# Rotary embedding over 16 batches: which batches form a pair, and where the first tile and the tables are loaded

## The chip, the cores and the metric

The kernel runs on one core of a Trainium2 chip. The metric is the device time of one execution in microseconds (us); before the change the median of three runs is 167.71 us (167.61 to 167.97). The core has five engines that this text calls PE (matrix products), DVE (vector), ACT (scalar), POOL (GpSimd) and SP (sync; here it only issues transfers). Transfers between DRAM and the on-chip memory run on 16 DMA engines. A transfer is put on the queue of the engine that issues it: SP's queue is q1 in the profile, ACT's is q10.

## The reference

A rotary position embedding. `x` is 16 batches of 512 rows of 16 heads by 64 numbers, 33.5 MB in float32; `cos` and `sin` are 512 by 32, 64 KB each, and are the same for all batches and heads.

```python
def reference(x, cos, sin, num_heads):
    batch, seq, dim = x.shape                    # 16, 512, 1024
    head_dim = dim // num_heads                  # 64
    half_dim = head_dim // 2
    x = x.reshape(batch, seq, num_heads, head_dim)
    x1, x2 = x[..., :half_dim], x[..., half_dim:]
    cos = cos[None, :, None, :]
    sin = sin[None, :, None, :]
    rotated = np.concatenate([x1 * cos - x2 * sin, x1 * sin + x2 * cos], axis=-1)
    return rotated.astype(np.float32)
```

Every number of `x` is read once and every number of the output is written once.

## The kernel before

**Tiles.** The work is cut into ten tiles (L40, L41). Tiles 0, 1, 8 and 9 hold one batch each (0, 1, 14 and 15): 4 rows of 1024 numbers on each of 128 partitions, 2 MB, each partition reading 16 KB in one piece. Tiles 2 to 7 hold two batches each (2 and 3, 4 and 5, up to 12 and 13): 8 rows per partition, 4 MB. In a pair, partition 2s belongs to the first batch and partition 2s + 1 to the second, and each reads 8 rows that lie together in DRAM, 32 KB in one piece. Two neighbouring batches are 2 MB apart. The 64 rows in all, in the order of the tiles, are numbered u = 0 to 63.

**Memory.** The tiles live in a ring of 40 rows, `x_sb` (RING, L43). Tiles 0 to 5 fill it. Tiles 6 to 9 take the places of earlier tiles: tile 6 that of tiles 0 and 1, tile 7 that of tile 2, and tiles 8 and 9 that of tile 3. The result of a row overwrites the row in the ring, and is stored from there.

**One row.** A row takes three steps. The product with cos goes to one of three buffers in PSUM, `t1_ps` (DVE, L313). The product of the swapped halves with sin (negative for the first half) goes to one of six buffers, `t2_sb`; POOL does it (L277), except in row 3 of each pair, where DVE does it (L306). Then the two are added: by DVE, straight into the ring (L324), or, in three rows of eight, by PE, which adds `t2_sb` to what stands in `t1_ps` by a product with the identity (L232), and ACT copies the sum to the ring (L198). DVE's product for row u waits until the buffer of row u - 3 is free: for ACT's copy of that row, or for its add.

**Tables.** `cos` and `sin` are loaded into `stage` with 4 rows on each partition, 512 bytes per partition and table. DVE copies cos to PSUM (L284) and waits for it before its first product. ACT makes the table of sin with both signs, `s1_sb` (L189, L190), and POOL waits for it before its first product. For the pairs, PE spreads both tables to 8 rows per partition by a product with a 0/1 matrix, `pick` (L215), and ACT makes `s2_sb` from the result (L193, L194). The spread relies on the order of the partitions in a pair, first and second batch in turn.

**Queues.** SP issues the first half of tile 0 (2 rows per partition, 1 MB), then cos, then sin (L165 to L167), and then the stores, each when the last row of its tile is done (L171, L173). ACT issues the second half of tile 0 (L177), the loads of tiles 1 to 5 (L183, L162), and then waits for sin. The semaphore of tile 0 counts 32, 16 for each half (L275, L299). The loads of tiles 6 to 9 stand between ACT's copies, at rows 17, 25 and 33 (`later`, L186, LAG being 10); ahead of each, ACT waits until the tiles whose place is taken have been stored (`sem_out`). What follows in ACT's program, the later copies among it, comes after that wait.

Of the kernel before, what the change touches and what calls it, by code (L numbers as in the profile page):

```python
# [6 lines left out]
def bass_split_heads_rope_kernel(  # L7
# [4 lines left out]
    num_heads: bass.AP,  # L12
    out: bass.AP,
):

# [6 lines left out]
    batch, seq, dim = x.shape  # L24
# [4 lines left out]
    R1 = seq // P  # L29
    R2 = 2 * R1  # L30
# [6 lines left out]
    COPY = mybir.ActivationFunctionType.Copy  # L37


    singles = (0, 1, batch - 2, batch - 1)  # L40
    tiles = [(b, R1 if b in singles else R2) for b in range(batch) if b in singles or b % 2 == 0]  # L41
    NT = len(tiles)
    RING = 5 * R2  # L43

    rows = [(t, r) for t, (_, n) in enumerate(tiles) for r in range(n)]
    NU = len(rows)
    EARLY = (NU - RING) // R2

# [17 lines left out]
    LAG = 10  # L66

    with ExitStack() as stack:
        x_sb = stack.enter_context(nc.sbuf_tensor([P, RING, H, 2, HALF], fp32))
        t2_sb = stack.enter_context(nc.sbuf_tensor([P, NT2, H, 2, HALF], fp32))  # L70
        stage = stack.enter_context(nc.sbuf_tensor([P, 2, R1 * HALF], fp32))
# [8 lines left out]
        sem_in = [stack.enter_context(nc.semaphore(f"in{t}")) for t in range(NT)]  # L80
        sem_out = [stack.enter_context(nc.semaphore(f"out{k}")) for k in range(EARLY)]
        sem_rest = stack.enter_context(nc.semaphore("rest"))
        sem_cos = stack.enter_context(nc.semaphore("cos"))
        sem_sin = stack.enter_context(nc.semaphore("sin"))
# [22 lines left out]
        x1 = x.rearrange("b (s r) d -> b s (r d)", r=R1)  # L107
# [4 lines left out]

        def in_dram(single, pairs, t):
            b, n = tiles[t]
            return single[b] if n == R1 else pairs[:, b:b + 2, :]

        def in_sbuf(t):
            b, n = tiles[t]
            k = b * R1 % RING
            return x_sb[:, k:k + n].rearrange("p n h t d -> p (n h t d)")  # L120

        def where(u):
# [24 lines left out]

        def stores_of(k):

            return sum(b * R1 // R2 == k for b, _ in tiles)  # L150

        HR = R1 // 2

        def load_half(eng, i):

            eng.dma_start(  # L156
                x_sb[:, i * HR:(i + 1) * HR].rearrange("p n h t d -> p (n h t d)"),
                x1[0, :, i * HR * dim:(i + 1) * HR * dim],
            ).then_inc(sem_in[0], 16)

        def load(eng, t):
            eng.dma_start(in_sbuf(t), in_dram(x1, x2, t)).then_inc(sem_in[t], 16)  # L162

        def on_sync(sp):
            load_half(sp, 0)  # L165
            for i, (table, sem) in enumerate(((cos, sem_cos), (sin, sem_sin))):
                sp.dma_start(stage[:, i, :], table.rearrange("(s r) d -> s (r d)", r=R1)).then_inc(sem, 16)  # L167
            for u in range(NU):
                t, r, k = where(u)
                if r == tiles[t][1] - 1:  # L170
                    wait_added(sp, u)  # L171
                    k = u // R2
                    sp.dma_start(in_dram(o1, o2, t), in_sbuf(t)).then_inc(sem_out[k] if k < EARLY else sem_rest, 16)  # L173
            sp.wait_ge(sem_rest, 16 * sum(stores_of(k) for k in range(EARLY, NU // R2)))

        def on_scalar(ae):
            load_half(ae, 1)  # L177
            later = {}
            for t, (b, n) in enumerate(tiles):
                if t == 0:  # L180
                    continue
                if b * R1 + n <= RING:
                    load(ae, t)  # L183
                else:

                    later.setdefault((b * R1 - RING) // R2 * R2 + R2 - 1 + LAG, []).append(t)  # L186
            ae.wait_ge(sem_sin, 16)
            sv = stage[:, 1, :].rearrange("s (r d) -> s r d", d=HALF)
            ae.activation(s1_sb[:, :, 0, :], sv, COPY, scale=-1.0)  # L189
            ae.activation(s1_sb[:, :, 1, :], sv, COPY).then_inc(sem_s, 1)  # L190
            ae.wait_ge(sem_t, 2)
            s2 = s2_sb[:].rearrange("p (k r) t d -> p k r t d", r=R1)
            ae.activation(s2[:, :, :, 0, :], pair_ps[:, :, 1, :, :], COPY, scale=-1.0)  # L193
            ae.activation(s2[:, :, :, 1, :], pair_ps[:, :, 1, :, :], COPY).then_inc(sem_s, 1)  # L194
            for u in range(NU):
                if PE2[u]:
                    ae.wait_ge(sem_e, n_pe[u])
                    ae.activation(xs[:, u % RING, :], t1_ps[:, u % NT1, :], COPY).then_inc(sem_a, 1)  # L198
                for t in later.get(u, ()):
                    k = (tiles[t][0] * R1 - RING) // R2  # L200
                    ae.wait_ge(sem_out[k], 16 * stores_of(k))
                    load(ae, t)

# [38 lines left out]
        def on_gpsimd(pl):  # L242
            pl.memset(ident[:], 1.0).then_inc(sem_i, 1)  # L243
            pl.wait_ge(sem_i, 1)
            pl.affine_select(  # L245
                out=ident[:],
                in_=ident[:],
                compare_op=mybir.AluOpType.is_equal,
                fill=0.0,
                base=0,  # L250
                pattern=[[-1, P]],
                channel_multiplier=1,
            ).then_inc(sem_i, 1)

            pl.memset(pick[:], 1.0).then_inc(sem_g, 1)
            pl.wait_ge(sem_g, 1)
            for k in range(2):
                pl.affine_select(  # L258
                    out=pick[:, k],
                    in_=pick[:, k],  # L260
                    compare_op=mybir.AluOpType.is_equal,
                    fill=0.0,
                    base=-k,
                    pattern=[[-2, P // 2], [0, 2]],
                    channel_multiplier=1,
                ).then_inc(sem_g, 1)
            for u in range(NU):
                if V2[u]:
                    continue
                t, r, k = where(u)  # L270
                if (t, r) == (0, 0):
                    pl.wait_ge(sem_s, 1)
                if (t, r) == (2, 0):
                    pl.wait_ge(sem_s, 2)
                pl.wait_ge(sem_in[t], 32 if t == 0 else 16)  # L275
                wait_t2_free(pl, u)
                pl.tensor_tensor(  # L277
                    t2_sb[:, u % NT2, :, :, :], swapped(k), over_heads(s_of(t, r)), mult
                ).then_inc(sem_p, 1)

        def on_vector(ve):
            ve.memset(zero[:], 0.0).then_inc(sem_z, 1)  # L282
            ve.wait_ge(sem_cos, 16)
            ve.tensor_copy(c1_ps, stage[:, 0, :].rearrange("s (r d) -> s r d", d=HALF)).then_inc(sem_c, 1)  # L284
            ve.wait_ge(sem_c, 1)
            ve.wait_ge(sem_w, NT1 * EH)

            def pair_tables():
                ve.wait_ge(sem_s, 2)
                row = pair_ps[:, V_ROW // R1, 1, V_ROW % R1, :]  # L290
                ve.tensor_scalar_mul(v_ps[:, 0, :], row, -1.0).then_inc(sem_c, 1)
                ve.tensor_copy(v_ps[:, 1, :], row).then_inc(sem_c, 1)

            first_v = V2.index(True)

            def mul(u):
                t, r, k = where(u)
                if r == 0:
                    ve.wait_ge(sem_in[t], 32 if t == 0 else 16)  # L299
                if (t, r) == (2, 0):  # L300
                    pair_tables()
                if u == first_v:
                    ve.wait_ge(sem_c, 3)
                if V2[u]:
                    wait_t2_free(ve, u)
                    ve.tensor_tensor(t2_sb[:, u % NT2, :, :, :], swapped(k), over_heads(v_ps), mult)  # L306
                if u >= NT1:
                    v = u - NT1
                    if PE2[v]:
                        ve.wait_ge(sem_a, n_pe[v])  # L310
                    else:
                        ve.wait_ge(sem_v, n_comb[v])
                ve.tensor_tensor(  # L313
                    t1_ps[:, u % NT1, :].rearrange("p (h d) -> p h d", d=HALF),
                    x_sb[:, k, :, :, :].rearrange("p h t d -> p (h t) d"),
                    c_of(t, r)[:, None, :].broadcast_to([P, 2 * H, HALF]),
                    mult,
                ).then_inc(sem_m, 1)

            def comb(u):  # L320
                t, r, k = where(u)
                ve.wait_ge(sem_m, u + 1)
                ve.wait_ge(sem_p, n_pool[u])  # L323
                ve.tensor_tensor(  # L324
                    xs[:, k, :],
                    t1_ps[:, u % NT1, :],
                    t2_sb[:, u % NT2, :, :, :].rearrange("p h t d -> p (h t d)"),
                    add,
                ).then_inc(sem_v, 1)

            for u in range(NU + LEAD):
                if u < NU:
                    mul(u)
                if u >= LEAD and not PE2[u - LEAD]:
                    comb(u - LEAD)
# [39 lines left out]
```

## Time and profile before

| | |
|---|---|
| median of three runs | 167.71 us |
| the profiled run | 167.97 us, span 166.6 us |
| bytes read and written | 33.69 MB and 33.55 MB |
| mean rate over the span | 404 GB/s |
| POOL busy | 136.4 us of the span |
| DVE busy | 130.1 us |
| first multiply on POOL begins | 24.7 us |
| first store issued | 35.4 us |
| last store issued | 160.2 us |

The span runs from the first to the last instruction of the profiled execution; the run's own time is 1.37 us more. An engine's busy time is the sum of its instructions; what an engine waited for is put down to the event that came last ahead of the instruction.

In a row of the groups, the parts are the line, the engine, the operation, what is written and what it is made from with their shapes, the number of instructions, then the busy time in us and the mean of one in ns, and then the idle time just before them and what ended most of it. In a row of the timeline, the first number is the start and the second the duration, both in us. In a row of a stretch of the span, the stretch's bounds and length are followed by the busy time of PE, PE's weight load, DVE, ACT and POOL, each with the number of instructions, then the granted clock of PE, the share of the 16 DMA engines that was busy, and GB/s. In the rows of the DMA queues, the numbers are packets, MB and the share of the 16 engines' span; in those of the issues, KB of each and the median time from issue to landing.

### The profile page before, as it was taken

How to read it: one execution, taken by the hardware profiler on the slowest of the kernel's cores; microseconds unless marked ns; L12 is line 12 of the kernel's file. 1: busy time of each engine (PE TensorE's matmuls, PEld its weight loads, DVE VectorE, ACT ScalarE, POOL GpSimd, SP SyncE). 2: the span in 40 equal slices, each digit the busy share in tenths (PEclk: the TensorE clock that was granted, in tenths of full speed). 3: DMA queues.
4: the chain of work that ended last, by engine and by line, in shares of the span. 5: the costliest groups of instructions: out<-in, count | busy, mean ns of one | idle time of the engine just before them, and what ended most of it. 6: DMA issues, size and time to landing. Idle time of an engine off the chain costs nothing.

```text
span 166.6 us, 569 instructions
## 1 busy us (share of the span) xinstructions
PE 70.1 (42%) x94; PEld 22.9 (14%) x94; DVE 130.1 (78%) x117; ACT 24.0 (14%) x26; POOL 136.4 (82%) x67
## 2 busy tenths in 40 slices
PE   6000013001749125936753484267744475496000
PEld 1000011001122102211212021111210122021000
DVE  0005004999499999999999999799999999998930
ACT  0300011000202220222040202220122211213000
POOL 5000009999999999999999999999999999999910
PEclk9955555555557995675598769876596965558555
DMA  5999999998999988989898989999998999489887
GB/s 146 439 426 492 408 396 472 401 480 342 425 449 433 409 358 378 488 270 496 299 456 388 496 386 472 429 413 401 441 476 382 437 445 456 181 378 472 346 374 319
DMA packets 3315, 67.26 MB, mean 404 GB/s; under 512 B 369, under 2 KB 625, under 8 KB 625
## 3 DMA queue, kind: packets, MB, share of 16 engines
q1 hardware_dynamic: 1872, 34.73, 49.5%
q10 hardware_dynamic: 1440, 32.51, 46.3%
q14 instruction: 3, 0.02, 0.0%
HBM read 33.69 MB, written 33.55 MB: 404 GB/s over the span
## 4 chain that ended last, share of the span: by engine, by line
DMA 29%; POOL 23%; DVE 16%; PE 12%; issue 11%; ACT 3%; ACTq 1%; SPq 0%; DVEq 0%; POOLq 0%
POOL t_sb L277 23%; DMA out_dram<-x_sb 15%; DMA stage<-in_sin_dram 13%; PE t_ps L232 12%; DVE t_ps L313 8%; DVE x_sb L324 6%; ACT x_sb L198 3%; DVE t_sb L306 1%; ACTq L162 1%; SPq L167 0%; SPq L156 0%; ACT s_sb L189 0%; ACT s_sb L190 0%; DVEq L323 0%; POOLq L146 0%
## 5 line engine op out<-in xcount | busy, mean ns | idle before, releaser
L277 POOL TENSOR_TENSOR t_sb<-x_sb,s_sb 128x1024 f32<-128x1024 f32 x58 | 134.1, 2375 | 21.6 <-ACT s_sb L190 21.6
L232 PE MATMUL t_ps<-t_sb,ident 128*128 128x512 f32 x84 | 65.3, 925 | 60.9 <-DVE t_ps L313 46.9
L324 DVE TENSOR_TENSOR x_sb<-t_ps,t_sb 128x1024 f32<-128x1024 f32 x43 | 52.3, 1217 | 11.6 <-POOL t_sb L277 11.6
L313 DVE TENSOR_TENSOR t_ps<-x_sb,pair_ps 128x1024 f32<-128x1024 f32 x48 | 57.7, 1222 | 3.5 <-ACT x_sb L198 3.4
L198 ACT ACTIVATE x_sb<-t_ps 128x1024 f32<-128x1024 f32 x21 | 21.5, 1024 | 105.1 <-PE t_ps L232 101.3
L232 PEld LDWEIGHTS t_ps<-t_sb,ident 128*128 128x128 f32 x84 | 21.0, 276 | 105.2 <-DVE t_ps L313 66.2
L313 DVE TENSOR_TENSOR t_ps<-x_sb,tab_ps 128x1024 f32<-128x1024 f32 x16 | 19.3, 1222 | 0.9 <-ACT x_sb L198 0.9
L215 PE MATMUL pair_ps<-stage,pick 128*128 128x256 f32 x4 | 2.0, 666 | 20.3 <-DMA stage<-in_sin_dram 20.3
L284 DVE COPY tab_ps<-stage 128x128 f32<-128x128 f32 x1 | 0.3, 295 | 13.0 <-DMA stage<-in_cos_dram 13.0
L306 DVE TENSOR_TENSOR t_sb<-x_sb,tab_ps 128x1024 f32<-128x1024 f32 x6 | 7.3, 1211 | 0.0
L215 PEld LDWEIGHTS pair_ps<-stage,pick 128*128 128x128 f32 x4 | 1.2, 323 | 21.3 <-issue 21.1
L208 PE MATMUL t_ps<-zero 128*128 128x512 bf16 x6 | 2.7, 630 | 1.3 <-DVE zero L282 1.3
L189 ACT ACTIVATE s_sb<-stage 128x128 f32<-128x128 f32 x1 | 0.3, 309 | 18.5 <-DMA stage<-in_sin_dram 18.5
L189 ACT ACT_TABLE_LOAD x1 | 1.3, 1283 | 4.3 <-issue 4.3
L258 POOL TENSOR_SCALAR_AFFINE_SELECT pick<-pick 128x128 f32<-128x128 f32 x2 | 1.4, 706 | 0.1
L208 PEld LDWEIGHTS t_ps<-zero 128*128 128x128 bf16 x6 | 0.7, 137 | 2.4 <-DVE zero L282 1.2
L282 DVE MEMSET zero<- 128x256 uint32 x1 | 0.3, 272 | 0.9 <-PEq L357 0.9
L193 ACT ACTIVATE s_sb<-pair_ps 128x256 f32<-128x256 f32 x1 | 0.4, 384 | 1.7 <-PE pair_ps L215 1.7
L243 POOL MEMSET ident<- 128x128 f32 x1 | 0.2, 206 | 0.3 <-POOLq L357 0.3
L194 ACT ACTIVATE s_sb<-pair_ps 128x256 f32<-128x256 f32 x1 | 0.4, 377 | 0.0
L245 POOL TENSOR_SCALAR_AFFINE_SELECT ident<-ident 128x128 f32<-128x128 f32 x1 | 0.3, 298 | 0.1
L357 POOL MEMSET const-float32-0.0<- 128x1 f32 x1 | 0.1, 99 | 0.3 <-issue 0.3
(7 smaller groups left out, 1.3 us busy)
## 6 DMA issues: line engine op xcount, KB each, us to landing
x_sb<-in_x_dram ACTq DMA_DIRECT2D x6, 4096.0 KB, 27.4
out_dram<-x_sb SPq DMA_DIRECT2D x6, 4096.0 KB, 19.1
out_dram<-x_sb SPq DMA_DIRECT2D x4, 2048.0 KB, 12.0
x_sb<-in_x_dram ACTq DMA_DIRECT2D x3, 2048.0 KB, 18.4
x_sb<-in_x_dram SPq DMA_DIRECT2D x1, 1024.0 KB, 7.4
x_sb<-in_x_dram ACTq DMA_DIRECT2D x1, 1024.0 KB, 8.4
stage<-in_cos_dram SPq DMA_DIRECT2D x1, 64.0 KB, 12.9
stage<-in_sin_dram SPq DMA_DIRECT2D x1, 64.0 KB, 22.4
```

What stands on the lines that cost most here:

```text
L162: eng.dma_start(in_sbuf(t), in_dram(x1, x2, t)).then_inc(sem_in[t], 16)
L189: ae.activation(s1_sb[:, :, 0, :], sv, COPY, scale=-1.0)
L193: ae.activation(s2[:, :, :, 0, :], pair_ps[:, :, 1, :, :], COPY, scale=-1.0)
L198: ae.activation(xs[:, u % RING, :], t1_ps[:, u % NT1, :], COPY).then_inc(sem_a, 1)
L208: pe.matmul(t1_ps[:, k, b * BANK:(b + 1) * BANK], zero[:, 0:P], zero[:], start=True, stop=True).then_inc(sem_w, 1)
L215: pe.matmul(pair_ps[:, k].rearrange("p c r d -> p (c r d)"), pick[:, k].rearrange("q s b -> q (s b)"), stage[:].rearrange("q c f -> q (c f)"),
L232: ins = pe.matmul(t1_ps[:, u % NT1, b * BANK:(b + 1) * BANK], ident[:], t2[:, b * BANK:(b + 1) * BANK], start=False, stop=True, skip_group ...
L258: pl.affine_select(out=pick[:, k], in_=pick[:, k], compare_op=mybir.AluOpType.is_equal, fill=0.0, base=-k, pattern=[[-2, P // 2], [0, 2]], ...
L277: pl.tensor_tensor(t2_sb[:, u % NT2, :, :, :], swapped(k), over_heads(s_of(t, r)), mult).then_inc(sem_p, 1)
L306: ve.tensor_tensor(t2_sb[:, u % NT2, :, :, :], swapped(k), over_heads(v_ps), mult)
L313: ve.tensor_tensor(t1_ps[:, u % NT1, :].rearrange("p (h d) -> p h d", d=HALF), x_sb[:, k, :, :, :].rearrange("p h t d -> p (h t) d"), c_of ...
L324: ve.tensor_tensor(xs[:, k, :], t1_ps[:, u % NT1, :], t2_sb[:, u % NT2, :, :, :].rearrange("p h t d -> p (h t d)"), add,).then_inc(sem_v, 1)
```

## The change

Two things change.

A pair joins batch b and batch b + 6: tiles 2 to 7 hold batches 2 and 8, 3 and 9, up to 7 and 13, which are 12 MB apart in DRAM instead of 2. Loads and stores both go by `in_dram`. The sizes of the tiles, the order of the partitions within a pair and the ring stay; as the place in the ring can't be computed from the batch any more, it is taken from `first`, the row at which a tile begins.

The first tile is loaded in one piece of 2 MB, on ACT's queue. The two tables follow it there, ahead of tile 1. SP issues stores alone. The semaphore of tile 0 counts 16.

```diff
-    singles = (0, 1, batch - 2, batch - 1)
-    tiles = [(b, R1 if b in singles else R2) for b in range(batch) if b in singles or b % 2 == 0]
+    FAR = (batch - 4) // 2
+    tiles = [(0, R1), (1, R1)] + [(2 + i, R2) for i in range(FAR)] + [(batch - 2, R1), (batch - 1, R1)]
     NT = len(tiles)
+    first = [sum(n for _, n in tiles[:t]) for t in range(NT)]
...
-            return single[b] if n == R1 else pairs[:, b:b + 2, :]
+            return single[b] if n == R1 else pairs[:, b:b + FAR + 1:FAR, :]
...
-            b, n = tiles[t]
-            k = b * R1 % RING
+            n = tiles[t][1]
+            k = first[t] % RING
...
-            return sum(b * R1 // R2 == k for b, _ in tiles)
-
-        HR = R1 // 2
-
-        def load_half(eng, i):
-
-            eng.dma_start(
-                x_sb[:, i * HR:(i + 1) * HR].rearrange("p n h t d -> p (n h t d)"),
-                x1[0, :, i * HR * dim:(i + 1) * HR * dim],
-            ).then_inc(sem_in[0], 16)
+            return sum(u // R2 == k for u in first)
...
         def on_sync(sp):
-            load_half(sp, 0)
-            for i, (table, sem) in enumerate(((cos, sem_cos), (sin, sem_sin))):
-                sp.dma_start(stage[:, i, :], table.rearrange("(s r) d -> s (r d)", r=R1)).then_inc(sem, 16)
             for u in range(NU):
...
         def on_scalar(ae):
-            load_half(ae, 1)
             later = {}
-            for t, (b, n) in enumerate(tiles):
-                if t == 0:
-                    continue
-                if b * R1 + n <= RING:
+            for t in range(NT):
+                if first[t] < RING:
                     load(ae, t)
                 else:
 
-                    later.setdefault((b * R1 - RING) // R2 * R2 + R2 - 1 + LAG, []).append(t)
+                    later.setdefault((first[t] - RING) // R2 * R2 + R2 - 1 + LAG, []).append(t)
+                if t == 0:
+                    for i, (table, sem) in enumerate(((cos, sem_cos), (sin, sem_sin))):
+                        ae.dma_start(stage[:, i, :], table.rearrange("(s r) d -> s (r d)", r=R1)).then_inc(sem, 16)
             ae.wait_ge(sem_sin, 16)
...
-                    k = (tiles[t][0] * R1 - RING) // R2
+                    k = (first[t] - RING) // R2
                     ae.wait_ge(sem_out[k], 16 * stores_of(k))
                     load(ae, t)
...
-                pl.wait_ge(sem_in[t], 32 if t == 0 else 16)
+                pl.wait_ge(sem_in[t], 16)
...
-                    ve.wait_ge(sem_in[t], 32 if t == 0 else 16)
+                    ve.wait_ge(sem_in[t], 16)
```

## The prediction

> **What bounds the kernel now.** I read the engine totals first, then the waits, then the DMA queues with their landing times, and last the stretches of the span.
>
> ```profile
> PE 70.1 (42%) x94; PEld 22.9 (14%) x94; DVE 130.1 (78%) x117; ACT 24.0 (14%) x26; POOL 136.4 (82%) x67
> ...
> q1 hardware_dynamic: 1872, 34.73, 49.5%
> q10 hardware_dynamic: 1440, 32.51, 46.3%
> ...
> L277 POOL TENSOR_TENSOR t_sb<-x_sb,s_sb 128x1024 f32<-128x1024 f32 x58 | 134.1, 2375 | 21.6 <-ACT s_sb L190 21.6
> ...
> x_sb<-in_x_dram SPq DMA_DIRECT2D x1, 1024.0 KB, 7.4
> x_sb<-in_x_dram ACTq DMA_DIRECT2D x1, 1024.0 KB, 8.4
> stage<-in_cos_dram SPq DMA_DIRECT2D x1, 64.0 KB, 12.9
> stage<-in_sin_dram SPq DMA_DIRECT2D x1, 64.0 KB, 22.4
> ```
>
> POOL's only long wait is 21.6 us, for the table that ACT makes out of sin. Sin takes 22.4 us to land though it is 64 KB, and it does not come alone: the trace lands cos at 14.5 us with tile 1 (14.7) and sin at 24.4 with tile 2 (24.6). The 16 table pieces per DMA engine on SP's queue take turns, one for one, with x pieces 32 and 64 times as long on ACT's queue. The timeline shows what that holds up, and how tightly POOL is packed afterwards: 58 multiplies from 24.73 to 158.8, 134.1 us of work in 134.1 us.
>
> ```profile
> 24.14 0.31 ACT L189 ACTIVATE s_sb<-stage 128x128 f32<-128x128 f32 x1 [18.51 <-DMA stage<-in_sin_dram]
> 24.35 0.29 ACT L190 ACTIVATE s_sb<-stage 128x128 f32<-128x128 f32 x1
> 24.73 11.58 POOL L277 TENSOR_TENSOR t_sb<-x_sb,s_sb 128x1024 f32<-128x1024 f32 x5 [21.65 <-ACT s_sb L190]
> ```
>
> So after a late start POOL sets the end. But the two DMA queues hold the 16 engines for 49.5 + 46.3 = 95.8% of the span, 159.6 us. The DMA engines are a second bound close behind. Their share, the number ahead of GB/s, shows where they rest:
>
> ```profile
> 0.00:4.00 4.00, 2.74 (x6) 0.73 (x6) 0.27 (x1) 0.00 (x0) 2.34 (x9) 1.00 0.51 135
> 36.00:60.00 24.00, 11.79 (x16) 3.91 (x16) 21.66 (x22) 3.53 (x4) 24.00 (x12) 0.66 0.99 417
> 60.00:66.00 6.00, 1.82 (x2) 0.84 (x3) 6.00 (x6) 0.56 (x1) 6.00 (x3) 0.72 0.93 396
> 66.00:138.00 72.00, 41.35 (x55) 12.83 (x53) 69.86 (x62) 14.34 (x14) 72.00 (x33) 0.74 1.00 419
> 138.00:150.00 12.00, 7.86 (x9) 2.68 (x10) 11.59 (x11) 1.67 (x2) 12.00 (x7) 0.50 0.76 325
> 150.00:159.00 9.00, 2.52 (x4) 0.70 (x3) 8.11 (x9) 1.41 (x2) 8.80 (x4) 0.69 1.01 433
> 159.00:163.00 4.00, 0.00 (x0) 0.00 (x0) 1.13 (x1) 0.00 (x0) 0.00 (x0) 0.50 0.76 320
> ```
>
> They rest 4 x 0.49 = 2.0 us before the first packets. After that they rest only where no store is ready and no load may be issued: 24 x 0.01 + 6 x 0.07 + 12 x 0.24 + 4 x 0.24 = 0.24 + 0.42 + 2.88 + 0.96 = **4.5 us**. The last is the gap between the store of tile 8 and that of tile 9, which waits for compute. These 4.5 us are what an earlier start can win, however much earlier it is.
>
> **Part 1, the tables and the first tile.** The tables leave SP's queue and follow the whole first tile on ACT's. Ahead of them on the same rings there is then only tile 0, whose halves land now at 0.8 + 7.4 = 8.2 and 0.8 + 8.4 = 9.2 us. Nothing rivals them, since SP's queue is empty until the first store. Lower bound for sin: with tile 0, 9.2. Upper bound: behind tile 1, as cos lands now, 1.25 + 12.9 = 14.2. I take 10.0: 128 KB at the 439 GB/s of the load-only stretch 12 to 36 is 0.3 us, the rest is for two more completions. POOL starts 24.73 - 24.11 = 0.62 after sin, so at **10.6 instead of 24.7, 14.1 us earlier** (9.8 to 14.8 by the bounds). One queue does not load slower than two: from 24.7 to 36 ACT's queue alone ran at full rate.
>
> ACT now issues 8 loads in a row: one of 0.40 (the half's row), two tables of 0.42 and 0.44 and five of 0.62 (3.08 in all, L162), so it is free at 5.2 instead of 4.3 and its 1.28 us table load ends by 6.5. Sin's landing at 10 hides that; without the cover it would cost 0.9. Tile 1 and all loads behind it come 0.3 us later; tile 1 (14.7) is needed after four multiplies, 10.6 + 4 x 2.32 = 19.9, so that costs nothing, and 0.3 us at most without that cover. On SP nothing stands ahead of the first store but its wait. The threshold of 16 in place of 32 and the tile arithmetic move no work: tile sizes, ring slots and the rows after which tiles 6 to 9 are issued stay.
>
> **What is late next.** If loads were never late, all of compute would move by 14.1 us and the last store, issued at 160.2, could be issued at 146.1. The DMA engines can't follow. Without the 4.5 us of rest the span is 166.6 - 4.5 = **162.1 us**. The last 2 MB store takes 6.4 us from issue to end (160.2 to 166.6), so it must be issued by 155.7 for that. Compute thus has 155.7 - 146.1 = 9.6 us to lose. It loses some, because ACT waits before L162 for old stores (rows 17, 25, 33), with its own later copies (L198) queued behind; DVE's multiply three rows on waits for those copies, and PE and POOL for DVE. Today only row 33 shows it: 3.8 us of "issue" before the copy at 104.87. Estimate for after, from about 430 GB/s shared between the queues (stores of 16 KB pieces get a third against 32 KB loads, pieces of equal size a half): the stores of tiles 0 and 1 land near 57, of tile 2 near 77, of tile 3 near 96, while ACT asks for them near 55, 71 and 90. ACT's stops of 2, 5 and 6 us delay the copy behind by 1, 4 and 4, of which DVE's lead eats about half. I take **6 us** of compute stall, bounds 0 and 13 (the stops in full). The last load lands at 137.6 in the trace, and near 141 by the same shares; it must land by 155.7 - 11.2 = 144.5 (four multiplies of 2.38, 1.6 for the last add and issue). So the last store is ready at 146.1 + 6 = 152.1 and at 141 + 11.2 = 152.2, both some 3.5 us before it must be, and DMA sets the end.
>
> **Part 2, pairs 12 MB apart.** Pieces stay 32 KB, as many of them, partitions in the same order; only the address of every second piece differs, in loads and stores. No row shows 12 MB. The nearest are loads of pairs 2 MB apart (12 to 36, 439 GB/s) and the one-batch store at the end (150 to 159, 433): no difference. I take 0. Lower bound: a gain of the packets that now run long, which my list of packet times sums to 3 us per engine. Upper bound: the trace's worst pair pieces, in patches around 72 and 82 us, took some 1.6 us instead of 1.21; if all 96 pair pieces of each engine did, 96 x 0.4 = 38 us.
>
> The Trainium skill speaks against this part: "DMA: Bandwidth & Descriptors", under latency and other measured facts, tells of row pitches of 2 MiB falling to 164 GB/s per direction and of 4 MiB to 103. At 2 MB the trace shows 439, so the rule's case, every partition one pitch further, isn't this one, where two batches alternate and each is read in sequence. By that rule the 50.3 MB of pairs, 117 us at 430 GB/s, would take 164/103 as long and the run 69 us more; no run here shows it.
>
> **Sum.** Span 162.1, plus 0.2 taken for the rests that stay. The profiled run took 167.97 for a span of 166.6, 1.37 around it: 162.3 + 1.4 = 163.7. It was 0.26 above the median of 167.71, so **163.4 us**.
>
> **Rivals.** *Compute still sets the end.* For it: DVE has 127 us of work in the 135.4 from 24.7 to 160.1 and can't catch up on a stall quickly. Against it: 9.6 us of room. At stalls of 12 us the end is 2.4 later: **165.8**. *The last load becomes the bound.* Stores that start 14 us earlier take turns with the loads earlier. If the last load lands 11.2 + 6.4 = 17.6 before an end that stays at 166.6, it lands at 149.0, 11.4 later than now: **167.7**, no change. Against it: all bytes that a later load lets pass are stores done sooner. *The far pairs cost the packets something*, the slower side: the 4.5 us are eaten at 4.5 / 96 = 47 ns per pair piece, 4%. At 10% the DMA bound grows by 96 x 0.12 = 11.5: **174.9**. Against it: load rows of one batch and of pairs run alike. *The tables don't come early* (behind tile 1): start 14.8, last store at 150.3 + 6 = 156.3, 0.6 late: **164.0**, hardly to be told from the forecast, so it counts there. *Long packets vanish with the new addresses*: 3 us less, **160.4**.
>
> **Chances.** DMA-bound end 0.62 (own range 162.2 to 164.5), compute end 0.18, last load 0.06, far pairs slower 0.09, long packets gone 0.05. A measurement here can tell 0.2%, 0.34 us. Faster: 0.62 + 0.18 + 0.05 = 0.85; same 0.06; slower 0.09. The range takes the first two: 161.9 to 166.5.
>
> **What would show it.** Sin landing near 10 us and POOL's first L277 near 10.6; the first store near 21; DMA share 0.98 or more from 4 us to the end; new waits of ACT before row 17, 25 and 33 loads, and idle of POOL in the middle, for the first time; a rest between the last two stores if compute sets the end. Wrong if 32 KB pieces are longer than 1.21 us on the whole, or if DMA rests after 150.

## The result and the profile after

The median after the change is **161.31 us** (161.22 to 161.68, six runs) against 167.66 us before (167.52 to 167.97, six runs): a ratio of 0.9625, with a 95% interval of 0.9612 to 0.9638. The kernel is faster by 6.35 us. The direction was forecast and so was the way there; the size was not, as 161.31 lies 0.6 us below the range of 161.9 to 166.5 and 2.1 us below the 163.4 forecast. The profiled run took 161.55 us for a span of 160.1. One of the four runs of c_far below was a slow one, 166.48 us, which its median leaves out and which its trace shows.

The start, in the timeline of the kernel after (start, duration, engine, line, what is written and read):

```profile
1.69 0.45 ACTq L176 DMA_DIRECT2D stage<-in_sin_dram  x1
...
8.96 0.31 ACT L179 ACTIVATE s_sb<-stage 128x128 f32<-128x128 f32 x1 [2.26 <-DMA stage<-in_sin_dram]
...
9.55 20.82 POOL L267 TENSOR_TENSOR t_sb<-x_sb,s_sb 128x1024 f32<-128x1024 f32 x9 [6.48 <-ACT s_sb L180]
...
20.19 0.38 SPq L163 DMA_DIRECT2D out_dram<-x_sb  x1
```

Sin now lands 7.2 us after its issue instead of 22.4, right behind tile 0, and POOL begins at 9.55 instead of 24.73, 15.2 us earlier. The first store is issued at 20.2 instead of 35.4, also 15.2 earlier. The end moved by 6.5 us only, and the totals and the DMA queues of the page say what holds it:

```profile
PE 75.0 (47%) x94; PEld 24.3 (15%) x94; DVE 130.2 (81%) x117; ACT 23.9 (15%) x26; POOL 136.4 (85%) x67
...
q10 hardware_dynamic: 1728, 33.69, 49.7%
q1 hardware_dynamic: 1440, 33.56, 48.8%
```

The engines run the same instructions as before. The DMA engines were taken for 95.8% of the span and now for 98.5%. Where they rest is in the stretches of the kernel after (bounds, length, busy time of the five engines, clock, DMA share, GB/s):

```profile
0.00:4.00 4.00, 2.74 (x6) 0.73 (x6) 0.27 (x1) 0.00 (x0) 2.33 (x9) 1.00 0.52 143
4.00:156.00 152.00, 72.22 (x88) 23.57 (x88) 129.92 (x116) 23.94 (x26) 134.12 (x58) 0.69 1.01 431
156.00:160.10 4.10, 0.00 (x0) 0.00 (x0) 0.00 (x0) 0.00 (x0) 0.00 (x0) 0.50 0.68 292
```

For 152 us on end nothing rests, at 431 GB/s. What used to be POOL's wait at the start is now a wait of compute in the middle, which costs nothing (the waits of POOL and DVE: who waits for whom, total us, times, longest):

```profile
POOL t_sb L267 <- ACT s_sb L180: 6.5, 1, 6.5
POOL t_sb L267 <- DVE x_sb L314: 3.6, 1, 3.6
POOL t_sb L267 <- DMA x_sb<-in_x_dram: 1.6, 1, 1.6
POOL t_sb L267 <- PE t_ps L222: 1.2, 1, 1.2
...
DVE t_ps L303 <- ACT x_sb L188: 10.3, 11, 4.3
```

POOL loses 3.6 + 1.6 + 1.2 = 6.4 us after its start, where it lost nothing before. Most of this is loads that land late. The 1.6 us are the first row of tile 7, which landed at 111.7. The 3.6 us, put down to DVE, end here:

```profile
140.82 9.27 POOL L267 TENSOR_TENSOR t_sb<-x_sb,s_sb 128x1024 f32<-128x1024 f32 x4 [3.61 <-DVE x_sb L314]
```

That is the first row of tile 9. In the program it waits for the load of tile 9, which landed at 140.8, and for a buffer that PE had freed by 134, but not for a DVE add. So 5.2 us are waits for loads, and 1.2 us come from ACT: it stops until the store of tile 3 has landed (92.5), its next copy is late, and DVE waits 4.3 us for it. That is the longest of DVE's waits for ACT's copies, which are 10.3 us in all, and were 4.3 in all before.

### The profile page after: what moved, and what is told of

Its sections match the earlier page's. It is cut to its first block, busy times and chain, and to the rows that moved or that the text cites. A ratio compares the mean times of both kernels' runs of the same rounds, so it can differ in the third digit from the quotient of the medians.

```text
span 160.1 us, 568 instructions
## 1 busy us (share of the span) xinstructions
PE 75.0 (47%) x94; PEld 24.3 (15%) x94; DVE 130.2 (81%) x117; ACT 23.9 (15%) x26; POOL 136.4 (85%) x67
## 4 chain that ended last, share of the span: by engine, by line
DVE 24%; DMA 23%; PE 18%; issue 12%; POOL 10%; ACT 5%; ACTq 2%; DVEq 0%; POOLq 0%
DMA out_dram<-x_sb 18%; PE t_ps L222 18%; DVE t_ps L303 13%; POOL t_sb L267 10%; DVE x_sb L314 10%; ACT x_sb L188 5%; DMA stage<-in_sin_dram 5%; DVE t_sb L296 2%; ACTq L155 1%; ACTq L176 0%; ACT s_sb L179 0%; ACT s_sb L180 0%; DVEq L313 0%; POOLq L146 0%; DVEq L148 0%
## 5 line engine op out<-in xcount | busy, mean ns | idle before, releaser
L222 PE MATMUL t_ps<-t_sb,ident 128*128 128x512 f32 x84 | 70.2, 989 | 61.7 <-DVE t_ps L303 51.5
L222 PEld LDWEIGHTS t_ps<-t_sb,ident 128*128 128x128 f32 x84 | 22.4, 294 | 109.1 <-DVE t_ps L303 68.9
## 6 DMA issues: line engine op xcount, KB each, us to landing
out_dram<-x_sb SPq DMA_DIRECT2D x4, 2048.0 KB, 14.7
```

Of the source, the lines that this page charges most:

```text
L222: ins = pe.matmul(t1_ps[:, u % NT1, b * BANK:(b + 1) * BANK], ident[:], t2[:, b * BANK:(b + 1) * BANK], start=False, stop=True, skip_group ...
```

## The missing two microseconds: long pieces

The forecast took the 4.5 us of DMA rest out of the span of 166.6 and so came to 162.1. The span is 160.1. The rest of the gain is in how long the DMA engines are busy at all. The trace keeps each piece: one of 32 KB takes 1.213 us as a rule, one of 16 KB 0.611, one of 8 KB 0.309. Added up per engine, the work of both kernels at those times is 156.2 us. What the pieces took beyond that is called *long pieces* below, summed over all and divided by 16. Before, it is 3.40 us; after, 1.48. The difference of 1.92 and the rests of 4.5 make 6.4 of the 6.5 us.

The long pieces stand in patches. In the kernel before the first is at the very start (0.77), one follows the first store (0.4), and two stand at 72 (0.9) and 80 (0.8). A patch can be seen in the stretches of before, as a rate far below 430 GB/s without a matching rest:

```profile
66.00:71.00 5.00, 4.57 (x7) 1.36 (x5) 4.75 (x5) 1.42 (x2) 5.00 (x4) 0.65 0.98 419
71.00:76.00 5.00, 2.30 (x3) 1.17 (x4) 5.00 (x6) 0.63 (x1) 5.00 (x3) 0.69 0.91 316
76.00:79.00 3.00, 1.48 (x2) 0.00 (x0) 2.59 (x3) 1.02 (x1) 3.00 (x2) 0.50 1.09 470
79.00:84.00 5.00, 3.35 (x4) 1.18 (x4) 5.00 (x5) 0.26 (x1) 5.00 (x3) 0.58 0.97 347
```

From 79 to 84 the engines are busy for 97% and move 347 GB/s: single pieces there took 1.3 to 2.8 us. The long pieces are mostly those of the queue that is already running, ahead of the first piece of the queue that starts: at 72 the 17 long store pieces begin from 70.7 to 72.5, and the load's first piece at 73.5; at 80 the 30 long pieces are the load's, from 80.0 on, and the store's first piece begins at 83.2. After the change the patches at 72 and 80 are gone; the first two remain. The forecast had charged these pieces to the kernel for good, save for a rival that put them down to the addresses. The experiments ask which part of the change takes them away, and why.

## The experiments

### Which part: e1_near and e2_far

Part 1 alone, with neighbouring batches in a pair:

```diff
-    tiles = [(0, R1), (1, R1)] + [(2 + i, R2) for i in range(FAR)] + [(batch - 2, R1), (batch - 1, R1)]
+    tiles = [(0, R1), (1, R1)] + [(2 + 2 * i, R2) for i in range(FAR)] + [(batch - 2, R1), (batch - 1, R1)]
...
-            return single[b] if n == R1 else pairs[:, b:b + FAR + 1:FAR, :]
+            return single[b] if n == R1 else pairs[:, b:b + 2, :]
```

> Part 1 alone: tile 0 in one piece and the tables behind it on ACT's queue, but pairs of neighbouring batches as before. Theory 1 (the long DMA pieces of before come where a queue starts again beside a running one, and vanish because no queue rests after the early start): 161.3 us as with the whole change, long pieces about 1.5 us per engine. Theory 2 (the far addresses shorten the pieces): long pieces stay at 3.4 us, so 161.3 + 1.9 = 163.2 us. In both POOL starts at 9.6.

Measured: 161.30 us, ratio 0.9618 (0.9605 to 0.9631), long pieces 1.32. This is the whole gain.

Part 2 alone, far pairs with the loads of before:

```diff
         def on_sync(sp):
+            load_half(sp, 0)
+            for i, (table, sem) in enumerate(((cos, sem_cos), (sin, sem_sin))):
+                sp.dma_start(stage[:, i, :], table.rearrange("(s r) d -> s (r d)", r=R1)).then_inc(sem, 16)
...
         def on_scalar(ae):
+            load_half(ae, 1)
             later = {}
-            for t in range(NT):
+            for t in range(1, NT):
...
```

> Part 2 alone: pairs 12 MB apart, with the first tile in halves on both queues and the tables behind SP's half as before. Theory 1: 167.7 us as before, POOL starts at 24.7, DMA rests of 4.5 us and long pieces of about 3.4 us stay. Theory 2: the rests stay but the long pieces fall to 1.5, so 165.8 us.

Measured: 167.54 us, ratio 0.9992 (0.9983 to 1.0001), long pieces 3.47, with the patches at 72 and 80 where they were. The distance of the two batches does nothing that these runs can tell, in either kernel. Theory 2 falls.

### Which piece of part 1: e3_halves and e5_behind2

Tile 0 in halves again, but the tables on ACT's queue behind its half:

```diff
         def on_sync(sp):
+            load_half(sp, 0)
...
-                if first[t] < RING:
+                if t == 0:
+                    load_half(ae, 1)
+                elif first[t] < RING:
                     load(ae, t)
...
```

> The whole change, but tile 0 again in two halves, one on each queue at once; the tables follow ACT's half. If only the place of the tables counts (both theories): sin lands within 1 us of tile 0, POOL starts near 9.6, 161.3 us within 0.3. If one piece of 2 MB on one queue is itself worth something (fewer long first pieces): up to 0.8 us more than 161.3.

Measured: 161.52 us, ratio 0.9633 (0.9617 to 0.9648), POOL's first multiply at 9.72, long pieces 1.37. Its interval overlaps that of e1_near and of the change. Halves or one piece can't be told apart.

The tables later on the same queue:

```diff
-                if t == 0:
+                if t == 2:
                     for i, (table, sem) in enumerate(((cos, sem_cos), (sin, sem_sin))):
```

> The whole change, but the two tables stand behind tile 2 on ACT's queue instead of behind tile 0, so they land near 24.5 as before and POOL starts near 25.2 with no rival queue and with far pairs. Theory 1: the rests and the long pieces of before come back, 167.7 to 168.3 us, long pieces about 3.4. Theory 2: the rests come back but the pieces stay short, about 166.2.

Measured: 167.63 us, ratio 0.9996 (0.9987 to 1.0004), POOL's first multiply at 24.38, long pieces 3.42. With one queue, one piece and far pairs, but tables that land with tile 2, the kernel is the old one to the last tenth. Its wait shows what counts:

```profile
24.38 6.96 POOL L267 TENSOR_TENSOR t_sb<-x_sb,s_sb 128x1024 f32<-128x1024 f32 x3 [21.31 <-ACT s_sb L180]
```

So the whole gain is the early landing of the tables, of which sin comes last, and the patches at 72 and 80 belong to the late start.

### How much of the early start is needed: e4_behind1

```diff
-                if t == 0:
+                if t == 1:
```

> The whole change, but the tables stand behind tile 1 on ACT's queue, so sin lands near 14.0 and POOL starts near 14.5, 5 us later than with the whole change. Theory 1 (the DMA engines set the end, and compute has room): the last store of the change is issued some 3.5 us before the stores ahead of it are through, and ACT's waits for stores shrink by what the start is later, so 161.3 to 161.9 us, no DMA rests in the middle, long pieces under 2. Rival (compute still sets the end after the change): 161.3 + 5 = 166.3.

Measured: 161.99 us (161.46 to 162.29), ratio 0.9658 (0.9641 to 0.9676); POOL starts at 14.64, 5.1 us later than after the change, for 0.7 us of time. That is clear of the change's 161.31 and just above the expected 161.9. ACT's waits for stores were to shrink, and they did not: its two longest are 4.5 and 7.2 us, 3.9 and 7.4 after the change. What went are POOL's waits for loads, as its rows come later: it loses 0.8 us after its start instead of 6.4. Long pieces are 1.67. The stores run out once, for 0.8 us near 140, where no rest was expected. An estimate from these 5.1 and 0.7 us: the DMA engines have some 4.4 us of room for a later start. The forecast had given 164.0 for this case: off by 2.0, as for the change itself, so the error may well be one term that is common to both.

### What the transfers alone take: c_far and c_near

Here all compute goes:

```diff
         def on_sync(sp):
-            for u in range(NU):
-                t, r, k = where(u)
-                if r == tiles[t][1] - 1:
-                    wait_added(sp, u)
-                    k = u // R2
-                    sp.dma_start(in_dram(o1, o2, t), in_sbuf(t)).then_inc(sem_out[k] if k < EARLY else sem_rest, 16)
+            for t, (b, n) in enumerate(tiles):
+                k = first[t] // R2
+                sp.wait_ge(sem_in[t], 16)
+                sp.dma_start(in_dram(o1, o2, t), in_sbuf(t)).then_inc(sem_out[k] if k < EARLY else sem_rest, 16)
...
```

> Transfers alone: all arithmetic and both tables are left out, each tile is stored as soon as it has landed, with pairs 12 MB apart. The output is x itself. If the DMA engines are the bound of the changed kernel and are full there, the same transfers alone take as long: 160.5 to 162 us. If compute costs the changed kernel something still, less than 160.

> Transfers alone as in c_far, with pairs of neighbouring batches, 2 MB apart. Theory 1: as c_far within 0.5 us, pieces of 32 KB alike. If the distance counts for the DMA engines when nothing else is in the way: c_far and c_near differ by more than 1 us.

Measured: 161.03 us for c_far, ratio 0.9602 (0.9587 to 0.9617), and 161.20 for c_near, ratio 0.9624 (0.9598 to 0.9650). Long pieces are 1.83 and 1.46. Near and far agree, and both agree with the changed kernel. Its compute costs it nothing that these runs can show; what is left in its time is these transfers, in this order and these sizes. The stretches of c_near (here POOL is the only engine in the row) read as those of the kernel after:

```profile
0.00:4.00 4.00, 0.20 (x4) 1.00 0.57 160
4.00:156.00 152.00, 0.00 (x0) 1.00 1.00 431
156.00:159.50 3.50, 0.00 (x0) 1.00 0.68 290
```

### What makes the patches: l_lag20, c_rest, c_total, c_nototal, c_keep

The first idea was that a queue which starts again beside a running one brings a patch.

```diff
-    LAG = 10
+    LAG = 20
```

> The whole change with LAG 20 in place of 10: tiles 6 to 9 are issued after rows 27, 35 and 43, so the load of tile 6 near 75 us instead of 53, when tile 5 has landed (73): ACT's queue rests while SP's runs on, and starts again beside it. Theory 1: a patch of long pieces of 0.4 to 0.9 us per engine near 77 for the first restart and one for each further one, so long pieces at 1.9 to 3.2 instead of 1.5; the time is longer by at least that, 161.7 to 163, and more where DMA rests because stores run out. Rival (long pieces have to do with compute's lateness or with the early stage, not with a restart): long pieces stay at 1.5.

Measured: 164.45 us, ratio 0.9812 (0.9794 to 0.9829). Long pieces rose to 2.44: 0.38 near 75, as expected, but 0.85 more from 84 to 90, with no rest of a queue before it. In the stretches both show as a low rate without a rest:

```profile
73.00:78.00 5.00, 1.98 (x4) 0.68 (x4) 5.00 (x5) 1.00 (x1) 5.00 (x3) 1.00 0.98 388
84.00:90.00 6.00, 3.87 (x6) 1.03 (x4) 5.74 (x6) 2.05 (x2) 6.00 (x3) 0.78 1.00 371
```

The rest of the loss is compute that came late: the DMA engines rest 2.3 us near 157, before the last store. POOL waited 11.3 us for x. This fits the idea in one place and not in the other.

The idea alone, without compute:

```diff
                 sp.wait_ge(sem_in[t], 16)
+                if t == 2:
+                    sp.wait_ge(sem_in[4], 16)
...
                     ae.wait_ge(sem_out[k], 16 * stores_of(k))
+                    if t == 6:
+                        ae.wait_ge(sem_out[2], 16)
```

> Transfers alone with near pairs as in c_near (all arithmetic and both tables left out), but each queue is made to rest once while the other runs on: the store of tile 2 waits until tile 4 has landed (SP's queue rests some 6 us before about 47), and the load of tile 6 waits until tile 3 has been stored (ACT's queue rests some 12 us, from about 66 to 79). The DMA engines as a whole should never rest. Theory 1 (a queue that starts again beside a running one brings a patch of long pieces): two new patches of 0.2 to 0.9 us per engine, at the two restarts, so long pieces at 2.0 to 3.2 us in place of 1.5 and 161.7 to 162.8 us in place of 161.1. Rival (the patches of before come from something else than the restart): no patch there, 161.1 us.

Measured: 161.20 us, ratio 0.9616 (0.9592 to 0.9640), long pieces 1.69. SP's queue rested from 40.1 to 57.9 and ACT's from 67.7 to 87.0, longer than ever in the kernel before, and neither start brought a patch. The first idea falls. What this kernel never had is a moment at which all DMA engines rest together, as before has from 62 to 64, ahead of both patches. The next one imitates that:

```diff
+            def pause(n):
+                for _ in range(n):
...
+                    ae.activation(t2_sb[:, 0].rearrange("p h t d -> p (h t d)"), xs[:, 39, :], COPY).then_inc(sem_a, 1)
...
                 sp.wait_ge(sem_in[t], 16)
+                if t == 2:
+                    sp.wait_ge(sem_in[5], 16)
+                if t == 3:
+                    sp.wait_ge(sem_a, 15)
...
                     ae.wait_ge(sem_out[k], 16 * stores_of(k))
+                    if t == 6:
+                        ae.wait_ge(sem_in[5], 16)
+                        pause(6)
                 load(ae, t)
+                if t == 6:
+                    pause(9)
```

> Transfers alone with near pairs (arithmetic and tables left out), made to run as the kernel before does from 60 us on: the store of tile 2 waits until tile 5 has landed, when no load is left, so all DMA engines rest for some 3 us; six copies of a row by ACT later the load of tile 6 starts beside that store alone, and nine copies after it the store of tile 3 beside that load alone. Theory 3 (the patches follow once all DMA engines have rested together and a queue starts beside them soon after): patches of 0.5 to 0.9 us per engine at the load of tile 6 and at the store of tile 3, long pieces 2.5 to 3.3 us. Theory 4 (the patches need the real compute beside the transfers, since two long rests of single queues brought none): long pieces stay at 1.5 to 1.8.

Measured: 167.23 us in one run, without any of the kernel's compute. Its stretches (here ACT and POOL, clock, DMA share, GB/s):

```profile
60.00:66.00 6.00, 2.99 (x3) 0.00 (x0) 1.00 0.63 268
66.00:72.00 6.00, 5.81 (x7) 0.00 (x0) 1.00 1.02 437
72.00:77.00 5.00, 4.87 (x5) 0.00 (x0) 1.00 0.90 315
77.00:81.00 4.00, 3.45 (x4) 0.00 (x0) 1.00 1.08 467
81.00:86.00 5.00, 0.00 (x0) 0.00 (x0) 1.00 1.02 341
```

After the common rest between 60 and 66 both patches are there: 315 GB/s where the load of tile 6 starts and 341 where the store of tile 3 starts, as 316 and 347 in the kernel before. Long pieces: 3.70, above the 3.3 expected. Theory 4 falls; the patches need none of the kernel's compute.

The control, with the store of tile 2 earlier (`sem_in[4]` in place of `sem_in[5]`):

> As c_total, but the store of tile 2 waits for tile 4 only, so the loads are still running when it starts and the DMA engines don't rest together; the load of tile 6 and the store of tile 3 start as there. Theory 3: long pieces at 1.5 to 1.8, no patch at the two starts. Theory 4: 1.5 to 1.8 here too. If patches stand here as in c_total, it is the start of one queue beside the other running alone that counts, at some places and not at others.

Measured: 170.48 us in one run, long pieces 3.88. This control failed: the stores ran out at 72.1 before the first piece of the load of tile 6 at 77.0, so all engines rested for 5 us after all, and patches stand at 77 and from 87 to 93. It can't tell the two readings apart. The control that holds has one more store ahead:

```diff
-                if t == 3:
+                if t == 4:
                     sp.wait_ge(sem_a, 15)
```

> Transfers alone as in c_nototal, where the stores ran out at 72 us and all engines rested before the load of tile 6 after all. Here the stores of tiles 2 and 3 are both issued when tile 4 has landed, so stores run on until the load of tile 6 starts beside them near 80 us, and the store of tile 4 is the one that waits for the fifteen copies of ACT and starts beside that load near 91. Theory 3 (patches follow where all engines have rested together before): none here, long pieces 1.5 to 1.8 us per engine. Theory 1 in a narrower form (a queue that starts beside one that runs alone with nothing else queued): patches at both starts as in c_total, long pieces 2.5 to 3.5.

Measured: 162.84 us in one run, long pieces 1.92, a little over the 1.8 expected. ACT's queue rested from 67.2 to 79.7 and SP's from 82.9 to 90.6, each started beside the other running alone, and there was no common rest. The stretches around the two starts:

```profile
66.00:78.00 12.00, 8.89 (x9) 0.00 (x0) 1.00 1.01 434
78.00:83.00 5.00, 4.88 (x5) 0.00 (x0) 1.00 0.99 426
83.00:89.00 6.00, 3.37 (x4) 0.00 (x0) 1.00 1.01 437
89.00:94.00 5.00, 0.00 (x0) 0.00 (x0) 1.00 0.97 419
```

No patch: 426 and 419 GB/s in place of 315 and 341. In these kernels of transfers alone the two patches come with a rest of all DMA engines, at the next starts of a queue, and not with the starts as such. One other thing differs between c_total and c_keep: the stores beside the two starts are those of tiles 2 and 3 in one, and 3 and 4 in the other. No run changes this alone; but in c_nototal the first patch came with no store under way.

## Why the prediction was right, and where it was wrong

**Where the time comes from: right.** Sin's late landing was the cause, the tables' place on the queue was the cure (e3_halves, e4_behind1, e5_behind2), and the DMA engines became the bound: the last store is issued at 151.5 us, while the stores ahead of it keep the engines full to the end.

**Tables and start: right in kind, and too cautious.** Sin was put at 10.0 and POOL at 10.6, and they came at 8.9 and 9.55, below their lower bounds of 9.2 and 9.8: the bounds took tile 0 to land at 9.2 as its later half did, and in one piece it landed at 8.6. The 1 us is worth little, as 5 us cost 0.7 in e4_behind1. The landing times that the prediction lists (14.5, 14.7, 24.4, 24.6, 137.6) are 0.3 us too late against its rows of the timeline, which changes next to nothing in its sums.

**What is late next: one of the two ways right, the other right in its number by luck.** Compute was to lose 6 us to ACT's waits for old stores, and POOL lost 6.4; but 5.2 of these are waits for loads, and ACT's waits account for 1.2. The stores were to land near 57, 77 and 96, and landed at 53.0, 73.3 and 92.5. The other way held: the last load was put at 141 and landed at 140.8, POOL took up its last four rows then, and the last store was to be ready at 152.2 and was issued at 151.5. Neither sets the time: the store ahead of the last one landed only at 155.3.

**Far pairs: right.** Taken as 0, and they are 0 in three comparisons: e1_near against the change, e2_far against before, c_near against c_far. The Trainium skill's rule on row pitch, weighed in the prediction from "DMA: Bandwidth & Descriptors", section "Latency and other measured facts", does not show at this access: with 12 MB between the two batches the kernel after moves 431 GB/s, where the prediction's estimate by the rule was 69 us more. The rule's own case, a large step from each partition to the next, no run here has.

**The sum: wrong.** The step that failed is "Without the 4.5 us of rest the span is 166.6 - 4.5 = 162.1 us". It takes the rests out and leaves the 159.6 us in which the engines were busy as they were. But 1.9 us of these were long pieces that come and go with the rests: 3.40 before, 1.48 after, 3.42 again in e5_behind2. The term that was missing, put at nothing in the sum, is the price that the common rest from 62 to 64 has after it ends; c_total shows such a price without the kernel's compute, 3.70 where c_near has 1.46. The 0.2 us added for rests that stay was not needed either, since nothing rests from 4 us to 156.

**The rival that gave 160.4** named the right quantity for the wrong reason. It let all long pieces, which it sized at 3 us, vanish with the new addresses and got a chance of 0.05, where part 2 alone leaves them at 3.47. Had the patches been lined up in time with the rest from 62 to 64, and not with addresses, they could have stood in the main sum.

**What stays open.** Why pieces run long after a common rest isn't shown; the runs show only when. l_lag20 has two patches (0.38 and 0.85) without a common rest before them, so such a rest is not the only way there. And it isn't always followed by one: after the rests of the kernel before near 144 and 161, when stores run alone to the end, the pieces are as short as ever. c_total, c_nototal and c_keep are single runs; their rates by stretch carry the reading, not their times. The patch at the first store, 0.2 to 0.7 us, and the 0.8 at the very start stand in every kernel and were not looked into.

## What to carry to other kernels

A small transfer on one queue, beside big pieces on another, advances by one small piece for each big one: put a table that everything waits for on the queue and at the place where nothing big can take turns with it, here behind the first tile. When DMA engines become the bound, compare the kernel with its transfers alone; here both take 161 us, so nothing is left to win in the arithmetic. And when a forecast takes rests out of a busy resource, check whether its busy time was longer because of those rests.

## What the runs showed of the hardware

- Two queues share the DMA engines piece by piece: sixteen 512 byte pieces per engine took 22.4 us to land beside pieces of 16 and 32 KB, and 7.2 us, most of it tile 0's, alone behind tile 0.
- After a common rest in the middle of the run, no piece under way on any of the 16 engines for 0.8 to 4.9 us, patches stand at two of the next queue starts (not at that of the store which ends the rest in the kernel before), in which 32 KB pieces take 1.3 to 3.1 us instead of 1.21, with or without compute, at a cost of 0.5 to 1.8 us per engine each (before, e2_far, e5_behind2, c_total, c_nototal). Rests of one queue of 8 to 19 us beside the other bring none in c_rest and c_keep; l_lag20 has two patches without a common rest.
- Reads and writes mixed run within 2% of reads alone: 431 GB/s from 4 to 156 us in the kernel after, 439 in the load-only stretch of before.
